# Rows of decays sent through DRAM and broadcast by DMA in place of selector products on TensorE

## The chip, the cores and the metric

The kernel runs on one core of a Trainium2 chip. The metric is the device time of one execution in microseconds (us). Before the change the median of three runs is 1075.29 us (1075.06 to 1076.16).

## The reference

One layer of a hybrid decoder, for a prompt of 512 tokens and 8 samples of 8 tokens each, width 1024, all in float32. After an RMS norm one projection gives the inputs of two recurrent mixers. The first is a Mamba-2 SSD with 16 heads (head size 64, state 128, 2 groups):

```
cum  = cumsum(lac)                                   # the decays of a chunk, per head
lmat = exp(where(causal, cum[t] - cum[s], -inf))
y_intra = (C_t . B_s) * lmat * dt_s   applied to x_s
y_inter = (C_t . h) * exp(cum[t])                    # h: state before the chunk
```

The second is an mLSTM with 4 heads (key 128, value 256), which has the same form with stabilised log gates: `dmat = exp(b[t] - b[s] + i[s] - m[t])` inside a chunk and `exp(b[t] + m_prev - m[t])` on the queries for the state. Both feed an output projection; then follow cross attention over 256 memory tokens and a SwiGLU, each with norms before and after. All new states are outputs too.

The part that matters here: for each head, one row of 512 numbers over the tokens (`cum` for SSD, `b - m` for mLSTM, called `sx`) must stand in all 128 partitions, since the matrix `cum[t] - cum[s]` has s on the partitions and t along the row. The exponential of the same row, for tokens 128 to 511, must stand in 64 partitions (SSD) or 128 (mLSTM).

## The kernel before, in words

Everything lies with features on the partitions and the 576 tokens (512 prompt, 64 sample) along the row. Projections go through `gemm` (L208): each float32 weight tile is split into a rounded part and a remainder (`split_w`, L178: a load into `raw` from SP's queue at L181, a cast on ScalarE at L191, a subtraction on VectorE at L198 or a DMA that accumulates at L196), and three matmuls (L215, L216, L218) make one product. `raw` has two buffers, the split weights three.

A scheduler sets the order on every engine at build time from a simulated timeline. Each engine, SP's DMA queue among them, then works strictly in that order and waits where something isn't ready. Hints in the code tie some instructions behind others (`issue_after`). One of them matters here: the matmuls of the value projection (`values`, L868, product at L882) are tied, by the list `steps_` at L925, behind the products of the SSD pairs (`inner[k]`, L712), so that they fill TensorE between the pairs in a written order. The projections of z are tied behind them in the same way (L1095, L1096).

Gates (L549 to L644, between about 60 and 95 us in the profile): the rows `cum` (16 heads) and `sx` (4 heads) are made in the pool `gates`, one row per partition. Lines 600 to 612 split each into three bfloat16 parts, stacked in `cumst` (80 x 576) and `sxst` (68 x 576); for each set of rows that is one memset on GpSimd, four operations on VectorE and three copies on ScalarE.

SSD of the prompt (`ssd_prompt`, L654, once for each of 2 groups): transposes, the products C.B (`cbs`), the states of the four chunks, and then 4 pairs of heads, 8 pairs in all. For each head of a pair, TensorE multiplies a selector column with `cumst` (L697), which puts the head's row into all 128 partitions of a PSUM bank `ps_l`. VectorE adds the negative decay of the partition and the causal mask, chunk by chunk, into `lm` (L700, four operations), ScalarE takes the exponential (L702), VectorE multiplies by `cbs` (L703). The tag `tmp` of `lm` has two buffers, so the two heads of a pair hold both. Matmuls make `ps_yi` from the pair (L710, 16 as recorded); after them the buffers are free. Then two more selector products (L715) put the pair's rows, tokens 128 to 511, into `ps_ec`, ScalarE takes their exponential into `ec` (L718, one buffer), VectorE multiplies by `ps_yn`, the product of the states (L723), and GpSimd adds to the output (L725).

mLSTM of the prompt (L957, 4 heads): a selector product with `sxst` (L960) gives `ps_d`; ScalarE takes its exponential into `qs` (L962), which GpSimd multiplies by the queries; VectorE adds gates and mask into `dm` (L966). `qs` and `dm` have two buffers each. The samples use the same stacks for tokens 512 to 575 (L780, L1013).

Of the kernel before, what the change touches and what calls it, by code (L numbers as in the profile page):

```python
# [11 lines left out]
F32 = mybir.dt.float32  # L12
F32R = mybir.dt.float32r
BF16 = mybir.dt.bfloat16
# [5 lines left out]
P = 128  # L20
T = 576
TP = 512
# [93 lines left out]
def build(nc, tc, ctx, I, O):  # L116
# [199 lines left out]
    c16 = ml.tile([P, NC16], BF16, name="c16")  # L316
    sel = C16("sel")
    CT = ml.tile([P, 5, 104], F32, name="CT")
    sxst = ml.tile([68, T], BF16, name="sxst")
    mrow = ml.tile([4, TS], F32, name="mrow")  # L320
    wendm = ml.tile([P, 5, 4], F32, name="wendm")
    scalem = ml.tile([P, 4, 4], F32, name="scalem")
# [121 lines left out]
    bcp = stb.enter_context(tc.tile_pool(name="bcp", bufs=1, reuse_waits="tile"))  # L444
    bc = bcp.tile([P, 4, T], F32, name="bc")
    cdup = bcp.tile([16, 2, TS], F32, name="cdup")
    cumst = bcp.tile([80, T], BF16, name="cumst")
    ncum = bcp.tile([P, 4, 16], F32, name="ncum")
    wend = bcp.tile([P, 5, 16], F32, name="wend")
    decp = bcp.tile([P, 4, 16], F32, name="decp")  # L450
# [98 lines left out]
    def row(name, n=68, dt=F32, tag=None):  # L549
        return gp_.tile([n, T], dt, name=name, tag=tag or name)  # L550
# [46 lines left out]
    V.tensor_copy(cdup, cum[0:16, TP:T].unsqueeze(1).to_broadcast([16, 2, TS]))  # L597
    A.copy(mrow, r2[:, TP:T])

    btt, d1t = row("btt", 48, BF16, tag="ig"), row("d1t", 48, tag="e1")  # L600
    for st_, src, n in ((cumst, cum[0:16, :], 16), (sxst, sx[r4, :], 4)):
        b0 = 32 if n == 4 else 0
        bt, d1 = btt[b0:b0 + n, :], d1t[b0:b0 + n, :]
        G.memset(st_, 0.0)
        V.tensor_copy(bt, src)
        A.copy(st_[0:n, :], bt)
        with tc.issue_after(sx_done.ins):
            V.tensor_tensor(d1, src, bt, op=ALU.subtract)
        V.tensor_copy(bt, d1)
        A.copy(st_[32:32 + n, :], bt)  # L610
        V.tensor_tensor(d1, d1, bt, op=ALU.subtract)
        A.copy(st_[64:64 + n, :], d1)
# [41 lines left out]
    def ssd_prompt(g):  # L654
        Bt, Ct = bc[:, g, :], bc[:, 2 + g, :]
        ps = MP("ps_bt")
        for c in range(4):
            TE.transpose(ps[:, c * P:(c + 1) * P], Bt[:, c * P:(c + 1) * P], ident)
        btok = sd.tile([P, 4, P], F32, name="btok", tag="btok")
        A.copy(btok, ps.rearrange("p (c k) -> p c k", c=4))  # L660
        ps = MP("ps_cb")
        for c in range(4):
            m = mm(ps[:, c * P:(c + 1) * P], Bt[:, c * P:(c + 1) * P], Ct[:, c * P:(c + 1) * P], start=True, stop=True,
                   skip_group_check=True)
        outer.append(m)
        cbs = sd.tile([P, 512], F32, name="cbs", tag="cbs")
        A.copy(cbs, ps)
        xdt, hs = [], [None]
        for c in range(4):
            ps = MP("ps_xt")  # L670
            for j in range(4):
                TE.transpose(ps[:, j * P:(j + 1) * P], xs[:, g * 4 + j, c * P:(c + 1) * P], ident)
            xd = sd.tile([P, 8, 64], F32, name="xdt", tag="xdt", bufs=4)
            V.tensor_tensor(xd, ps.rearrange("p (h k) -> p h k", h=8),
                            CT[:, c, 32 + 8 * g:40 + 8 * g].unsqueeze(2).to_broadcast([P, 8, 64]), op=ALU.mult)
            xdt.append(xd)
            xe = sd.tile([P, 8, 64], F32, name="xe", tag="xe", bufs=1)
# [12 lines left out]
        for j in range(4):  # L690
            jj = g * 4 + j
            psi = MP("ps_yi")
            lms = []
            for k in range(2):
                h = 2 * jj + k
                psb = MP("ps_l")
                mm(psb, sel[:80, h:h + 1].to_broadcast([80, P]), cumst[:, 0:TP], start=True, stop=True)  # L697
                lm = sd.tile([P, 512], F32, name="lm", tag="tmp", bufs=2)
                for c in range(4):
                    V.scalar_tensor_tensor(lm[:, c * P:(c + 1) * P], psb[:, c * P:(c + 1) * P], ncum[:, c, h:h + 1],  # L700
                                           C16("maskp"), op0=ALU.add, op1=ALU.add)
                exps.append(A.activation(lm, lm, AF.Exp))  # L702
                mults.append(V.tensor_tensor(lm, lm, cbs, op=ALU.mult))  # L703
                lms.append(lm)
                if len(mults) == 8:
                    G.tensor_copy(sd.tile([P, 1], F32, name="lm0"), lm[:, 0:1])

            for c in range(4):
                for k in (1, 0):
                    m = mm(psi[64 * k:64 * k + 64, c * P:(c + 1) * P], xdt[c][:, 2 * j + k, :], lms[k][:, c * P:(c + 1) * P],  # L710
                       start=True, stop=True, skip_group_check=True)
            inner.append(m)  # L712
            pse = MP("ps_ec")
            for k in range(2):
                mm(pse[64 * k:64 * k + 64, 0:384], sel[:80, 2 * jj + k:2 * jj + k + 1].to_broadcast([80, 64]),  # L715
                   cumst[:, P:TP], start=True, stop=True, skip_group_check=True)
            ec = sd.tile([P, 384], F32, name="ec", tag="ec", bufs=1)
            A.activation(ec, pse[:, 0:384], AF.Exp)  # L718
            psn = MP("ps_yn")
            for c in range(1, 4):  # L720
                mm(psn[:, (c - 1) * P:c * P], hs[c][:, 2 * j:2 * j + 2, :].rearrange("p h k -> p (h k)"),
                   Ct[:, c * P:(c + 1) * P], start=True, stop=True, skip_group_check=True)
            V.tensor_tensor(ec, ec, psn[:, 0:384], op=ALU.mult)  # L723
            V.scalar_tensor_tensor(y[:, jj, 0:TP], xs[:, jj, 0:TP], PAR("dskip", jj), psi, op0=ALU.mult, op1=ALU.add)
            G.tensor_tensor(y[:, jj, P:TP], y[:, jj, P:TP], ec, op=ALU.add)  # L725
# [50 lines left out]
    for g in range(2):  # L776
        psb = BP("ps_ls")
        pb3 = psb.rearrange("p (h t) -> p h t", h=8)
        for h in range(8):
            mm(psb[:, h * TS:(h + 1) * TS], sel[:80, 8 * g + h:8 * g + h + 1].to_broadcast([80, P]), cumst[:, TP:T],  # L780
               start=h == 0, stop=h == 7, skip_group_check=True)
# [174 lines left out]

    for h in range(4):  # L957
        q, k = qk[:, h, :], qk[:, 4 + h, :]
        psb = MP("ps_d")
        mm(psb, sel[:68, h:h + 1].to_broadcast([68, P]), sxst[:, 0:TP], start=True, stop=True)  # L960
        qs = mp_.tile([P, 384], F32, name="qs", tag="qs", bufs=2)
        A.activation(qs, psb[:, P:TP], AF.Exp)  # L962
        G.tensor_tensor(qs, qs, q[:, P:TP], op=ALU.mult)
        dm = mp_.tile([P, 512], F32, name="dm", tag="dm", bufs=2)
        for c in range(4):
            V.scalar_tensor_tensor(dm[:, c * P:(c + 1) * P], psb[:, c * P:(c + 1) * P], CT[:, c, 64 + h:65 + h],  # L966
                                   C16("maskp"), op0=ALU.add, op1=ALU.add)
        A.activation(dm, dm, AF.Exp)
        pss = MP("ps_s")
# [40 lines left out]
    psb = BP("ps_ds")  # L1010
    pb3 = psb[:, 0:256].rearrange("p (h t) -> p h t", h=4)
    for h in range(4):
        mm(psb[:, h * TS:(h + 1) * TS], sel[:68, h:h + 1].to_broadcast([68, P]), sxst[:, TP:T], start=h == 0, stop=h == 3,  # L1013
           skip_group_check=True)
    es = vt4_[:, 4128:4384].rearrange("p (h t) -> p h t", h=4)
    A.activation(es, pb3, AF.Exp)
# [1460 lines left out]
```

## Time and profile before

| | |
|---|---|
| median of the runs | 1075.29 us |
| the profiled execution | 1074.69 us |
| its span in the profile | 1072.9 us |
| granted TensorE clock, mean | 0.999 |
| moved by DMA | 181.74 MB, mean 169 GB/s |

The span is the stretch that the profile covers; the execution's own time is 1.8 us longer. PE is TensorE's matmul, PEld its weight load, DVE VectorE, ACT ScalarE, POOL GpSimd, SPq the queue on which SP issues DMAs. A row of a group gives line, engine, operation, output and inputs, shapes, count and durations. In views by time, the first column is the start in us from the beginning of the span, the second the duration of a merged piece, and a bracket at the end says how long the engine sat idle before it and what released it. In the chain of waits, the second column is the slot, the time that passed to the next piece. Matmuls are pipelined: the recorded duration of one is longer than its slot.

### The profile page before, as it was taken

To read this page: it belongs to the slowest core of one execution; us is meant where nothing else is said; L and a number is where in the kernel's file an instruction comes from. 1 tells how busy PE (TensorE), PEld (TensorE's weight loads), DVE (VectorE), ACT (ScalarE), POOL (GpSimd) and SP (SyncE) were. 2 spreads that over 40 slices of the span, in tenths; PEclk is the share of its full clock that TensorE was granted. 3 is DMA by queue.
4 is the path that set the end of the run, shared out by engine and by line. 5 is a ranking of instruction groups with operands and counts; after the bars stand their busy time and mean duration, and the time that the engine had idled before them with its cause. 6 is when DMAs were issued, how large, how long until landed. Compare 5 with 4: busy or idle time off the path is not lost.

```text
span 1072.9 us, 20686 instructions
## 1 busy us (share of the span) xinstructions
PE 1063.1 (99%) x8096; PEld 1011.0 (94%) x8096; DVE 757.7 (71%) x1523; ACT 608.9 (57%) x1102; POOL 231.0 (22%) x305
## 2 busy tenths in 40 slices
PE   9999999999999999999999999999999999999997
PEld 8999887778999999999999989999999999999997
DVE  6798775658878774758755556766467887787556
ACT  7778523345654555655555445645566566656654
POOL 0454543313213111000154201100011111111000
PEclk9999999999999999999999999999999999999999
DMA  6776544425655349642468775743476687578532
GB/s 209 176 162 132 158 134 172 147 89 168 196 150 152 106 143 330 235 170 98 158 213 288 265 256 176 254 124 98 133 179 137 160 188 178 114 191 188 144 119 89
DMA packets 58965, 181.74 MB, mean 169 GB/s; under 512 B 6604, under 2 KB 12108, under 8 KB 58356
## 3 DMA queue, kind: packets, MB, share of 16 engines
q1 hardware_dynamic: 42884, 138.22, 38.7%
q0 software_dynamic: 15408, 41.43, 19.7%
q8 instruction: 63, 1.03, 0.4%
q10 hardware_dynamic: 576, 0.79, 0.2%
q14 instruction: 34, 0.28, 0.1%
HBM read 159.75 MB, written 20.65 MB: 168 GB/s over the span
## 4 chain that ended last, share of the span: by engine, by line
PE 98%; DVE 0%; DMA 0%; POOL 0%; issue 0%; ACT 0%; SPq 0%; DVEq 0%
PE ps_in L215 7%; PE ps_in L218 7%; PE ps_in L216 7%; PE ps_v L882 5%; PE ps_g L1946 3%; PE ps_u L1946 3%; PE ps_g L1945 3%; PE ps_o L218 3%; PE ps_o L216 3%; PE ps_u L1947 3%; PE ps_g L1947 3%; PE ps_o L215 3%; PE ps_u L1945 3%; PE ps_dn L1945 2%; PE ps_dn L1947 2%; PE ps_dn L1946 2%
## 5 line engine op out<-in xcount | busy, mean ns | idle before, releaser
L215 PE MATMUL ps_in<-uh,whi 128*128 128x320 f32 (+1 forms) x544 | 162.6, 299 | 0.0
L218 PE MATMUL ps_in<-uh,wlo 128*128 128x320 f32 (+1 forms) x544 | 161.6, 298 | 0.0
L216 PE MATMUL ps_in<-ul,whi 128*128 128x320 f32 (+1 forms) x544 | 161.1, 296 | 0.0
L191 ACT CAST whi<-raw 128x1024 fp32r<-128x1024 f32 (+1 forms) x104 | 105.4, 1015 | 93.3 <-PE ps_in L216 21.5
L198 DVE TENSOR_TENSOR wlo<-raw,whi 128x1024 fp32r<-128x1024 f32 (+2 forms) x97 | 95.3, 983 | 63.7 <-ACT whi L191 63.0
L215 PEld LDWEIGHTS ps_in<-uh,whi 128*128 128x128 f32 x544 | 102.3, 188 | 1.9 <-issue 0.8
L218 PEld LDWEIGHTS ps_in<-uh,wlo 128*128 128x128 f32 x544 | 102.2, 188 | 1.9 <-issue 1.3
L216 PEld LDWEIGHTS ps_in<-ul,whi 128*128 128x128 f32 x544 | 102.4, 188 | 0.5
L196 POOL DMA_DIRECT2D wlo<-win x31 | 27.2, 877 | 80.2 <-ACT wlo L195 69.9
L1945 PE MATMUL ps_g<-b,whi 128*128 128x288 f32 x144 | 42.4, 295 | 0.0
L1946 PE MATMUL ps_g<-b,whi 128*128 128x288 f32 x144 | 42.3, 294 | 0.0
L1946 PE MATMUL ps_u<-b,whi 128*128 128x288 f32 x144 | 42.2, 294 | 0.0
L1945 PE MATMUL ps_u<-b,whi 128*128 128x288 f32 x144 | 42.2, 294 | 0.0
L1905 DVE TENSOR_TENSOR wlo<-sw,whi 128x1024 fp32r<-128x1024 f32 (+1 forms) x26 | 29.6, 1139 | 16.8 <-ACT whi L1904 16.8
L1918 ACT CAST whi<-rawx 128x1024 fp32r<-128x1024 f32 (+1 forms) x26 | 25.6, 986 | 26.2 <-PE ps_dn L1946 13.3
L1895 ACT CAST whi<-raw 128x1024 fp32r<-128x1024 f32 (+1 forms) x26 | 25.6, 985 | 22.8 <-PE ps_g L1946 11.8
L215 PE MATMUL ps_xo<-qh,whi 128*128 128x288 f32 x128 | 38.2, 301 | 0.0
L216 PE MATMUL ps_xo<-ql,whi 128*128 128x288 f32 x128 | 37.8, 297 | 0.0
L218 PE MATMUL ps_o<-mixm_h,wlo 128*128 128x256 f32 (+1 forms) x128 | 37.5, 293 | 0.0
L216 PE MATMUL ps_o<-mixm_l,whi 128*128 128x256 f32 (+1 forms) x128 | 37.5, 293 | 0.0
L218 PE MATMUL ps_xq<-u2h,wlo 128*128 128x320 f32 (+1 forms) x128 | 37.5, 294 | 0.0
L218 PE MATMUL ps_o<-mixs_h,wlo 128*128 128x320 f32 (+1 forms) x128 | 37.4, 293 | 0.0
(788 smaller groups left out, 3855.6 us busy)
## 6 DMA issues: line engine op xcount, KB each, us to landing
raw<-win SPq DMA_DIRECT2D x35, 512.0 KB, 4.4
raw<-wout SPq DMA_DIRECT2D x17, 512.0 KB, 4.2
raw<-wxq SPq DMA_DIRECT2D x13, 512.0 KB, 4.7
raw<-wgate SPq DMA_DIRECT2D x13, 512.0 KB, 3.3
raw<-wup SPq DMA_DIRECT2D x13, 512.0 KB, 4.7
wlo<-win POOLq DMA_DIRECT2D x24, 256.0 KB, 5.6
kva<-vc SPq DMA_DIRECT2D x11, 512.0 KB, 5.9
raw<-wv SPq DMA_DIRECT2D x10, 512.0 KB, 4.0
```

What stands on the lines that cost most here:

```text
L191: casts.append(A.copy(hi[:, :n], raw[:, :n]))
L196: accs.append(G.dma_start(lo[:, a:b], src[:, a:b], accum_op=ALU.add))
L198: e.tensor_tensor(lo[:, a:b], raw[:, a:b], hi[:, a:b].bitcast(F32), op=ALU.subtract)
L215: mm(ps, wh, ah, start=i == 0, stop=False)
L216: products.append(mm(ps, wh, al, start=False, stop=False))
L218: m = mm(ps, tiles[order[c]][1], xh(order[c], t0, n), start=False, stop=c == len(tiles) - 1)
L882: mm(ps, a, b, skip_group_check=True, **kw)
L1895: s.c1 = A.copy(s.h1[:, s.all], s.r1[:, s.all])
L1905: V.tensor_tensor(s.l2[:, s.all], sw[:, s.all], s.h2[:, s.all].bitcast(F32), op=ALU.subtract)
L1945: mm(ps, wh, b[0][k], start=start and k == 0, stop=False, skip_group_check=True)
L1946: mm(ps, wh, b[1][k], start=False, stop=False, skip_group_check=True)
L1947: m = mm(ps, wl, b[0][k], start=False, stop=k == nk - 1, skip_group_check=True)
```

## The change

The prompt's rows no longer go through the selector. Four DRAM tiles are added: `cum_d` (16 x 512), `ecum_d` (16 x 384), `sx_d` (4 x 512) and `esx_d` (4 x 384). ScalarE takes the exponentials of the rows once, ahead, into `ecr`; SP stores the four. Where `ps_l`, `ps_ec` and `ps_d` stood, SP now loads the row of a head, or of its exponential, broadcast over the partitions, straight into `lm`, `ec`, `qs` and `dm`; the additions of VectorE then work in place on SBUF. The stacks `cumst` and `sxst` shrink to the 64 sample tokens, and with them the conversions that fill them. `ecr` takes over the buffer `ig`, and `btt` gets one of its own.

```diff
-    sxst = ml.tile([68, T], BF16, name="sxst")
+    sxst = ml.tile([68, TS], BF16, name="sxst")
...
-    cumst = bcp.tile([80, T], BF16, name="cumst")
+    cumst = bcp.tile([80, TS], BF16, name="cumst")
...
-    btt, d1t = row("btt", 48, BF16, tag="ig"), row("d1t", 48, tag="e1")
-    for st_, src, n in ((cumst, cum[0:16, :], 16), (sxst, sx[r4, :], 4)):
+    cum_d, ecum_d, sx_d, esx_d = [dr.tile([n, w], F32, name=k) for n, w, k in
+                                  ((16, TP, "cum_d"), (16, 384, "ecum_d"), (4, TP, "sx_d"), (4, 384, "esx_d"))]
+    ecr = row("ecr", 36, tag="ig")
+    A.activation(ecr[0:16, 0:384], cum[0:16, P:TP], AF.Exp)
+    A.activation(ecr[r4, 0:384], sx[r4, P:TP], AF.Exp)
+    S.dma_start(cum_d, cum[0:16, 0:TP])
+    S.dma_start(ecum_d, ecr[0:16, 0:384])
+    S.dma_start(sx_d, sx[r4, 0:TP])
+    S.dma_start(esx_d, ecr[r4, 0:384])
+    btt, d1t = row("btt", 48, BF16, tag="btt"), row("d1t", 48, tag="e1")
+    for st_, src, n in ((cumst, cum[0:16, TP:T], 16), (sxst, sx[r4, TP:T], 4)):
...
-                psb = MP("ps_l")
-                mm(psb, sel[:80, h:h + 1].to_broadcast([80, P]), cumst[:, 0:TP], start=True, stop=True)
                 lm = sd.tile([P, 512], F32, name="lm", tag="tmp", bufs=2)
+                S.dma_start(lm, cum_d[h:h + 1, :].to_broadcast([P, TP]))
                 for c in range(4):
-                    V.scalar_tensor_tensor(lm[:, c * P:(c + 1) * P], psb[:, c * P:(c + 1) * P], ncum[:, c, h:h + 1],
+                    V.scalar_tensor_tensor(lm[:, c * P:(c + 1) * P], lm[:, c * P:(c + 1) * P], ncum[:, c, h:h + 1],
                                            C16("maskp"), op0=ALU.add, op1=ALU.add)
...
-            pse = MP("ps_ec")
+            ec = sd.tile([P, 384], F32, name="ec", tag="ec", bufs=1)
             for k in range(2):
-                mm(pse[64 * k:64 * k + 64, 0:384], sel[:80, 2 * jj + k:2 * jj + k + 1].to_broadcast([80, 64]),
-                   cumst[:, P:TP], start=True, stop=True, skip_group_check=True)
-            ec = sd.tile([P, 384], F32, name="ec", tag="ec", bufs=1)
-            A.activation(ec, pse[:, 0:384], AF.Exp)
+                S.dma_start(ec[64 * k:64 * k + 64, :], ecum_d[2 * jj + k:2 * jj + k + 1, :].to_broadcast([64, 384]))
...
-        psb = MP("ps_d")
-        mm(psb, sel[:68, h:h + 1].to_broadcast([68, P]), sxst[:, 0:TP], start=True, stop=True)
         qs = mp_.tile([P, 384], F32, name="qs", tag="qs", bufs=2)
-        A.activation(qs, psb[:, P:TP], AF.Exp)
+        S.dma_start(qs, esx_d[h:h + 1, :].to_broadcast([P, 384]))
         G.tensor_tensor(qs, qs, q[:, P:TP], op=ALU.mult)
         dm = mp_.tile([P, 512], F32, name="dm", tag="dm", bufs=2)
+        S.dma_start(dm, sx_d[h:h + 1, :].to_broadcast([P, TP]))
         for c in range(4):
-            V.scalar_tensor_tensor(dm[:, c * P:(c + 1) * P], psb[:, c * P:(c + 1) * P], CT[:, c, 64 + h:65 + h],
+            V.scalar_tensor_tensor(dm[:, c * P:(c + 1) * P], dm[:, c * P:(c + 1) * P], CT[:, c, 64 + h:65 + h],
                                    C16("maskp"), op0=ALU.add, op1=ALU.add)
```

The two lines for the samples (L780, L1013) read the whole of the smaller stacks.

More of the change, by code (lines that the diff above doesn't have):

```diff
@@ L598, in build @@
     A.copy(mrow, r2[:, TP:T])
-    btt, d1t = row("btt", 48, BF16, tag="ig"), row("d1t", 48, tag="e1")
-    for st_, src, n in ((cumst, cum[0:16, :], 16), (sxst, sx[r4, :], 4)):
+    cum_d, ecum_d, sx_d, esx_d = [dr.tile([n, w], F32, name=k) for n, w, k in
[9 more added lines that the diff above has]
+    for st_, src, n in ((cumst, cum[0:16, TP:T], 16), (sxst, sx[r4, TP:T], 4)):
         b0 = 32 if n == 4 else 0
-        bt, d1 = btt[b0:b0 + n, :], d1t[b0:b0 + n, :]
+        bt, d1 = btt[b0:b0 + n, 0:TS], d1t[b0:b0 + n, 0:TS]
         G.memset(st_, 0.0)
@@ L779, in build @@
         for h in range(8):
-            mm(psb[:, h * TS:(h + 1) * TS], sel[:80, 8 * g + h:8 * g + h + 1].to_broadcast([80, P]), cumst[:, TP:T],
+            mm(psb[:, h * TS:(h + 1) * TS], sel[:80, 8 * g + h:8 * g + h + 1].to_broadcast([80, P]), cumst,
                start=h == 0, stop=h == 7, skip_group_check=True)
@@ L1012, in build @@
     for h in range(4):
-        mm(psb[:, h * TS:(h + 1) * TS], sel[:68, h:h + 1].to_broadcast([68, P]), sxst[:, TP:T], start=h == 0, stop=h == 3,
+        mm(psb[:, h * TS:(h + 1) * TS], sel[:68, h:h + 1].to_broadcast([68, P]), sxst, start=h == 0, stop=h == 3,
            skip_group_check=True)
```

## The prediction

> **What bounds the kernel now.** I read the page first, then a table by stage over the part that the diff touches, then the chain of waits in that part, and last the order of VectorE's work there.
>
> ```profile
> span 1072.9 us, 20686 instructions
> PE 1063.1 (99%) x8096; PEld 1011.0 (94%) x8096; DVE 757.7 (71%) x1523; ACT 608.9 (57%) x1102; POOL 231.0 (22%) x305
> ```
>
> TensorE is busy for 1063.1 of 1072.9 us. Busy time alone says little when matmuls overlap, so the stage table (time; then busy us of PE, PEld, DVE, ACT, POOL; granted clock, share of the DMA engines, GB/s) is needed too:
>
> ```profile
> 130.00:160.00 30.00, 30.00 (x247) 25.93 (x246) 23.11 (x49) 9.79 (x17) 11.99 (x8) 1.00 0.43 130
> 160.00:190.00 30.00, 30.00 (x178) 22.11 (x177) 16.59 (x30) 9.00 (x14) 12.50 (x10) 1.00 0.45 159
> 190.00:220.00 30.00, 30.00 (x151) 22.85 (x150) 18.64 (x29) 10.08 (x14) 7.80 (x6) 1.00 0.43 149
> 220.00:260.00 40.00, 40.00 (x291) 34.70 (x290) 29.76 (x67) 24.75 (x40) 12.13 (x20) 1.00 0.46 141
> ```
>
> From 130 to 260 us, where the eight head pairs of the SSD run between projection products, PE has no gap at all, at full granted clock. The other engines have room, and the DMA engines are not half used. A matmul that is taken out here shortens the kernel by its slot, as long as the rest of the work stays in time for TensorE's fixed order.
>
> **What is removed.** Three kinds of selector products go. First their count (tile view), then their slots (chain of waits: start, us, work); a slot is what TensorE gives up, while the recorded duration overlaps its neighbours.
>
> ```profile
> L697 PE MATMUL ps_l<-cumst,c x16: 377/390/392, 129.4 to 243.8; 80*128 80x512 bf16 x16
> L715 PE MATMUL ps_ec<-cumst,c x16: 327/328/328, 138.9 to 248.2; 80*64 80x384 bf16 x16
> L960 PE MATMUL ps_d<-sxst,c x4: 380/381/383, 249.3 to 343.3; 68*128 68x512 bf16 x4
> ```
> ```profile
> 215.88 0.17 PE ps_ec L715 x2
> ...
> 221.08 0.45 PE ps_l L697 x2
> ```
>
> Two of the ps_l take 0.45 us, so 16 take 16 x 0.22 = 3.5 us. The two halves of ps_ec run side by side, 0.17 for both, so eight pairs take 8 x 0.165 = 1.3. Four of ps_d, of the same width, take 4 x 0.22 = 0.9. The sum is 5.7 us. The upper end adds the time in which the weight load before ps_l sat idle (its line's view says `issue`), if that goes as well:
>
> ```profile
>   issue: 2.6, 10
> ```
>
> That is PEld's idle time, most of it under running matmuls, so I do not take it; it makes the best case 8.3.
>
> ScalarE loses twelve exponentials and VectorE nothing but its wait for PSUM. The additions and masks keep their count and shapes and only read SBUF in place of PSUM; I cost that at nothing, VectorE having 7 to 13 us free in each stage above. The PSUM banks that are set free may help the order, and I count nothing for it.
>
> **What is added: the refills.** The rows go out once by four stores, early: the decays are there when their conversion starts (72.1, a row further below), long before the first ps_l at 129.4. SP then issues 16 broadcasts of 128 x 512 floats for lm, 16 of 64 x 384 for ec, four of 128 x 512 for dm and four of 128 x 384 for qs: 4.2 + 1.6 + 1.0 + 0.8 = 7.6 MB. Over some 215 us (129 to 343) that is 35 GB/s beside the 130 to 159 in the table, which fits shares of 0.43 to 0.46. Transfers as such are not the matter; latency is.
>
> For dm and qs there are two buffers, and the four heads lie 31 us apart (249.3 to 343.3): hidden. The one ec buffer is free from the add of one pair to the product of the next, and the pairs lie 9 us or more apart (below): hidden unless the queue is stuck. The lm buffers are the tight case. There are two, one pair needs both, and both are held until that pair's last product. Where PE could put the next rows into PSUM ahead of that, the new DMA cannot be issued before it. So: how long is it today from the last product of a pair (ps_yi) to the first addition (L700) of the next? First the chain of waits, then VectorE in order of time:
>
> ```profile
> 138.03 1.02 PE ps_yi L710 x16
> ...
> 152.35 1.02 PE ps_yi L710 x16
> ...
> 214.85 1.02 PE ps_yi L710 x16
> ...
> 227.71 1.02 PE ps_yi L710 x16
> ...
> 238.52 1.02 PE ps_yi L710 x16
> ...
> 247.32 1.07 PE ps_yi L710 x16
> ```
> ```profile
> 143.52 1.13 DVE L700 SCALAR_TENSOR_TENSOR lm<-ps_l,ncum,c 128x128 f32<-128x128 f32 x4 [2.78 <-PE ps_l L697]
> 150.88 0.68 DVE L703 TENSOR_TENSOR lm<-lm,cbs 128x512 f32<-128x512 f32 x1
> 156.97 2.15 DVE L700 SCALAR_TENSOR_TENSOR lm<-ps_l,ncum,c 128x128 f32<-128x128 f32 x8
> 167.52 2.16 DVE L700 SCALAR_TENSOR_TENSOR lm<-ps_l,ncum,c 128x128 f32<-128x128 f32 x8 [1.40 <-PE ps_l L697]
> 221.35 2.16 DVE L700 SCALAR_TENSOR_TENSOR lm<-ps_l,ncum,c 128x128 f32<-128x128 f32 x8 [3.78 <-PE ps_l L697]
> 234.19 2.16 DVE L700 SCALAR_TENSOR_TENSOR lm<-ps_l,ncum,c 128x128 f32<-128x128 f32 x8 [1.34 <-PE ps_l L697]
> 243.61 2.16 DVE L700 SCALAR_TENSOR_TENSOR lm<-ps_l,ncum,c 128x128 f32<-128x128 f32 x8 [2.38 <-PE ps_l L697]
> 245.69 1.47 DVE L703 TENSOR_TENSOR lm<-lm,cbs 128x512 f32<-128x512 f32 x2
> ```
>
> The six gaps are 143.52 - 139.05 = 4.5, then 3.6, 5.5 (the one whose pair is not shown), 5.5, 5.5 and 4.1 us. (The first pair of each group finds its buffers free long before.) Behind them lies a second reserve: from the end of the pair's last mask product (L703) to its ps_yi. At the first it is 152.35 - 151.56 = 0.8, at the last 247.32 - 247.16 = 0.2; the six, in order, are 0.8, 0.1, 0.9, 2.3, 0.8, 0.2. A refill that lands within gap plus reserve, 5.3, 3.7, 6.3, 7.8, 6.2 and 4.2 us after its release, costs TensorE nothing. How long will it take? No such DMA is in the trace; these are the nearest (KB, median us from issue to landing):
>
> ```profile
> raw<-wv SPq DMA_DIRECT2D x10, 512.0 KB, 4.0
> c<-c SPq DMA_DIRECT2D x8, 516.0 KB, 6.7
> ...
> o_ssmp<-hs SPq DMA_DIRECT2D x2, 256.0 KB, 3.0
> ```
>
> The 256 KB store lands in 3.0 us, and a pair of lm is as much as one 512 KB load, 4.0. The second lm is needed only 1.1 us after the first (four additions), so the pair should do as today. I take 3.0 for the first and 4.0 for the second, by size: nothing late. The upper end is 6.7, the longest row; the lower end, below nothing, would be an earlier chain, but TensorE, already full, could not run faster by it. The Trainium skill, DMA: Bandwidth & Descriptors, section "Anatomy of one DMA", fits 2.0 us plus bytes over 436 GB/s; by it 256 KB take an estimated 2.6 us, and the sum stays as it is. No run here shows that fit for this size; the row above says 3.0.
>
> **What is added and moved early on.** The two exponentials over the rows come where the conversions stand, from 72 us on, among casts and SiLUs. Each can cost a change of ScalarE's table there and back:
>
> ```profile
> 80.00:90.00 10.00, 10.00 (x68) 8.61 (x67) 9.75 (x23) 9.62 (x16) 4.76 (x10) 1.00 0.82 110
> ```
> ```profile
> 90.04 1.28 ACT L635 ACT_TABLE_LOAD   x1
> ```
> ```profile
> L606 ACT COPY cumst<-btt x1: 672/672/672, 72.1 to 72.1; 16x576 bf16<-16x576 bf16 x1
> ```
>
> Four loads are 5.1 us, the two exponentials about 0.6 each by the 0.67 of a row this wide. Against it stand six copies of 576 columns (0.67 each) that shrink to 64: by columns alone 0.6 each, 3.6 in all; some of a copy is fixed, so an estimate of half, 1.8, is nearer. At worst ScalarE gets 5.1 + 1.2 - 1.8 = 4.5 us more work in a stage where it is busy 9.62 of 10; at best, with no table load, 2.4 less. VectorE, at 9.75 of 10, gets its eight operations on those rows shortened the same way, which is a relief. Weights are converted a tile or more ahead, so I take no cost on TensorE. The stores are four SP issues among loads that wait for buffers anyway.
>
> **The sum.** The profiled execution took 1074.69 us, so 1074.69 - 5.7 = 1069.0; it lay 0.6 below the median of the runs, so 1069.6 beside 1075.29.
>
> **Rivals.** First, slower: SP, being in order, has a refill standing behind a weight load that waits for its buffer. In the stretch from 60 to 360 us:
>
> ```profile
> SPq L181 <- DVE wlo L198: 100.1, 23, 14.4
> ```
>
> The mean wait is 100.1 / 23 = 4.35 us. With one such wait ahead of each of the six tight refills the first lm lands 7.35 us after its release, late by 2.1, 3.6, 1.0, 0, 1.1 and 3.1: 11.0 us. TensorE cannot fill that in, since a written order ties the value products behind the pairs (L881). Result 1069.6 + 11.0 = 1080.6. It decides where release to landing passes 6.3 us, at which the lateness eats the 5.7. For it: SP waits this way often. Against: the scheduler that fixes SP's order gives the earlier-written lm precedence when its buffer is free.
>
> Second, slower still: the gaps above cannot be used, because the scheduler fills them with other VectorE work and the landing is exposed in full. Each refill then costs 3.0 less the reserve: 2.2 + 2.9 + 2.1 + 0.7 + 2.2 + 2.8 = 12.9, so 1082.5. The Trainium skill, DMA: Bandwidth & Descriptors, section "Rules for kernel authors", asks for a DMA to be issued early and waited for late; two buffers for a pair do not allow that here. Against: VectorE stood idle in five of the six gaps, 1.3 to 3.8 us, waiting for ps_l.
>
> Third, no change: refills take the 6.7 of the slowest row, late by 1.4, 3.0, 0.4, 0, 0.5 and 2.5 = 7.8 us, so 1077.4, just within what counts as no change. Against: an lm has half the bytes.
>
> Fourth, also no change: ScalarE's table loads delay converted weights by the full 4.5, so 1074.1. Against: it takes both changes of table, and a TensorE that is out of weights at once.
>
> **How the numbers follow.** What a measurement can tell from no change is about 0.2%, 2.15 us. Forecast 0.50 (faster); refills behind SP's waits 0.22 and exposed landing 0.08 (slower, 0.30 together); slow landing 0.12 and table loads 0.08 (within, 0.20 together). The range runs from 1067.0 (the 2.6 us of weight-load idle gone too) to 1081.0, past the first rival; only the second lies beyond. The forecast's own range is 1067.0 to 1072.
>
> **What would show it.** Right: PE's count lower by 36, no PE gap from 130 to 355, waits of VectorE for ps_l replaced by like waits for the DMA of lm, release to landing of lm 3 to 4 us, pairs about as far apart as now. Wrong: PE idle before ps_yi, released by L703 or lm; SP waits ahead of the lm broadcasts; landings over 6 us; new table loads between 68 and 90 us with PE waiting on whi or wlo. If PE is dense and the time has not fallen, other products would have grown, and my view of slots would be wrong.

## The result, and the profile after

| | before | after |
|---|---|---|
| median of 6 runs each | 1075.82 us (1075.06 to 1076.96) | 1092.76 us (1090.43 to 1094.43) |
| the profiled execution | 1074.69 us | 1090.43 us |
| its span | 1072.9 us | 1088.7 us |
| granted TensorE clock, mean | 0.999 | 0.991 |

The ratio is 1.0156, with a 95% interval of 1.0143 to 1.0169: the change makes the kernel slower by 16.8 us. The prediction said 1069.6, and 1081.0 at the upper end. In the two profiled executions nearly all of the loss lies between 80 and 400 us: the first product of the gates' transposes (`ps_ct`) is 0.6 us later than before, the first of the output projection (`ps_o`) 15.3 us (384.1 before, 399.4 after), and the cross attention still 15.2 (496.7, 511.9). The whole span is 15.8 us longer; the last 0.6 us come later.

The head of the page of the kernel after:

```profile
span 1088.7 us, 20696 instructions
PE 1068.7 (98%) x8060; PEld 1014.3 (93%) x8060; DVE 761.3 (70%) x1523; ACT 606.4 (56%) x1096; POOL 230.7 (21%) x305
```

TensorE has its 36 products fewer (8060 beside 8096), yet it is busy for 5.6 us longer, and idle for 20.0 us (1088.7 - 1068.7) beside 9.8. The stage table, in the columns of the prediction, shows where:

```profile
130.00:160.00 30.00, 26.21 (x229) 21.89 (x230) 21.34 (x36) 7.27 (x12) 14.89 (x12) 0.97 0.42 124
160.00:190.00 30.00, 30.00 (x175) 25.07 (x176) 19.45 (x37) 7.38 (x11) 3.85 (x5) 0.91 0.58 189
190.00:220.00 30.00, 29.93 (x138) 20.15 (x137) 17.24 (x23) 9.84 (x13) 15.52 (x11) 1.00 0.58 191
220.00:260.00 40.00, 38.59 (x260) 32.53 (x258) 27.89 (x56) 18.55 (x28) 10.30 (x16) 1.00 0.64 177
```

Before, all of these had PE full and a clock of 1.00. Now PE stands still for 3.8 us in the first stretch, and in the second, where it is busy all the time, the clock is 0.91. The waits of PE from 60 to 420 us (what waited, for what: us in all, times, longest) name the stops; before, this view was empty:

```profile
PE ps_yi L718 <- DVE lm L711: 3.8, 1, 3.8
PE ps_in L215 <- DVE tmp L1093: 2.3, 1, 2.3
PE ps_in L215 <- DVE tmp L1137: 0.9, 1, 0.9
PE ps_hts L1078 <- DVE hns L1075: 0.9, 1, 0.9
PE ps_en L634 <- ACT CT L628: 0.8, 1, 0.8
PE ps_nh L1053 <- DMA c<-c: 0.7, 2, 0.4
PE ps_ct L626 <- ACT r L595: 0.3, 1, 0.3
```

A stop can cost more than its length. TensorE's own order of time around the longest:

```profile
155.83 0.28 PE L215 MATMUL ps_in<-uh,whi 128*128 128x256 f32 x1
159.89 1.97 PE L718 MATMUL ps_yi<-lm,xdt 128*64 128x128 f32 x16 [3.79 <-DVE lm L711]
...
163.88 0.41 PE L218 MATMUL ps_in<-uh,wlo 128*128 128x256 f32 x1
164.10 0.41 PE L215 MATMUL ps_in<-uh,whi 128*128 128x256 f32 x1
...
165.43 0.28 PE L216 MATMUL ps_in<-ul,whi 128*128 128x256 f32 x1
165.54 0.28 PE L218 MATMUL ps_in<-uh,wlo 128*128 128x256 f32 x1
```

Behind the stop the projection's products start 0.22 us apart and are recorded with 0.41; from 165.2 on they are 0.11 apart, with 0.28. For 5.3 us TensorE ran at half rate, so 2.6 us went on top of the 3.8. Over the stages from 60 to 400 us the shares of the clock that are missing from 1.00 add up to 6.8 us, beside 9.7 us of stops: 16.5 together, and 10.8 when the 5.7 us of slots that went are taken off. This counts a little twice: the record of half rate around this stop runs from 158.38 to 165.21 us, and until 159.89 TensorE stood still. The other 4.4 of the 15.2, and some 0.7 more for what is counted twice, lie spread over slots that grew without a stop, and come back under what stays open.

Now the cause of the long stop. VectorE and GpSimd in order of time, after:

```profile
149.06 1.14 DVE L708 SCALAR_TENSOR_TENSOR lm<-lm,ncum,c 128x128 f32<-128x128 f32 x4 [1.81 <-DMA lm<-cum_d]
150.12 0.68 DVE L801 TENSOR_TENSOR xs<-yds,ps_yis 128x512 f32<-128x512 f32 x1
150.71 6.18 DVE L708 SCALAR_TENSOR_TENSOR lm<-lm,ncum,c 128x128 f32<-128x128 f32 x4
150.91 7.78 POOL L826 TENSOR_TENSOR h<-h,vt 128x1024 f32<-128x1024 f32 x4 [1.94 <-PE ps_hs L818]
157.15 2.68 DVE L711 TENSOR_TENSOR lm<-lm,cbs 128x512 f32<-128x512 f32 x2
```

The refill was 1.81 us late for VectorE, as the prediction expected of it. Then four additions take 1.14 us, and the next four, of the same shape, 6.18: those run while GpSimd multiplies `h`. Of the four, the first took 0.35 us and the other three 2.02 to 2.03. The mask product at 157.15 took 2.08. And the same beside the same work before the change:

```profile
141.80 8.08 POOL L821 TENSOR_TENSOR h<-h,vt 128x1024 f32<-128x1024 f32 x4
...
146.00 2.07 DVE L703 TENSOR_TENSOR lm<-lm,cbs 128x512 f32<-128x512 f32 x1
```

There the additions that read `ps_l` from PSUM kept their 0.34 us (143.52, 1.13 for four, shown ahead of the result), but the mask product, which reads both its inputs from SBUF, took 2.07 in place of 0.68. So a slowed mask product occurs without the change too; the slowed additions do not. The price of moving an input to SBUF stood in the trace of before, between two rows that the prediction quoted.

The tile view of `lm` and of `dm`, after (count, then ns min/median/max; then us and times that an engine sat idle until that DMA; then release to landing):

```profile
L708 DVE SCALAR_TENSOR_TENSOR lm<-lm,ncum,c x64: 339/346/2032, 110.5 to 248.3; 128x128 f32<-128x128 f32 x64
...
  DMA lm<-cum_d: 10.2, 7
...
DMA to landing us min/median/max: 3.1/3.5/6.0
```
```profile
  DMA dm<-sx_d: 7.3, 4
...
DMA to landing us min/median/max: 3.4/4.0/7.5
```

The landings are what was forecast, and VectorE waits 10.2 us for `lm`'s DMA where it had waited 11.7 for `ps_l`. Only the maximum of 2032 ns shows what went wrong; the median of the additions is nearly unchanged (346 ns, 340 before).

### The profile page after: what moved, and what is told of

It reads as the page before. It is cut to its first block, busy times and chain, and to the rows that moved or that the text cites. A ratio compares the mean times of both kernels' runs of the same rounds, so it can differ in the third digit from the quotient of the medians.

```text
span 1088.7 us, 20696 instructions
## 1 busy us (share of the span) xinstructions
PE 1068.7 (98%) x8060; PEld 1014.3 (93%) x8060; DVE 761.3 (70%) x1523; ACT 606.4 (56%) x1096; POOL 230.7 (21%) x305
## 4 chain that ended last, share of the span: by engine, by line
PE 83%; DMA 6%; DVE 5%; ACT 2%; issue 1%; POOL 1%; SPq 1%; DVEq 0%; ACTq 0%
PE ps_in L215 4%; PE ps_in L218 4%; PE ps_v L887 4%; PE ps_in L216 4%; PE ps_g L1950 3%; PE ps_u L1950 3%; PE ps_g L1949 3%; PE ps_o L218 3%; PE ps_o L216 3%; PE ps_u L1951 3%; PE ps_g L1951 3%; PE ps_u L1949 3%; PE ps_o L215 3%; PE ps_dn L1949 2%; PE ps_dn L1951 2%; PE ps_dn L1950 2%
## 5 line engine op out<-in xcount | busy, mean ns | idle before, releaser
L191 ACT CAST whi<-raw 128x1024 fp32r<-128x1024 f32 (+1 forms) x104 | 105.1, 1014 | 115.4 <-PE ps_in L216 27.2
L216 PE MATMUL ps_in<-ul,whi 128*128 128x320 f32 (+1 forms) x544 | 163.6, 301 | 0.0
L215 PE MATMUL ps_o<-mixm_h,whi 128*128 128x256 f32 (+1 forms) x128 | 37.4, 292 | 0.0
```

The source lines that it names most:

```text
L191: casts.append(A.copy(hi[:, :n], raw[:, :n]))
L215: mm(ps, wh, ah, start=i == 0, stop=False)
L216: products.append(mm(ps, wh, al, start=False, stop=False))
```

## The experiments

Theory A, formed from these rows: latency of the refills is not the matter; the loss is (1) additions that slow down beside GpSimd, (2) early exponentials that make ScalarE load tables ahead of `CT`, (3) waits and order on VectorE around the start of the mLSTM, each enlarged by the half rate. The rival: the round trip through DRAM is too slow for the two `lm` buffers. All runs are in one table; "over" is (ratio - 1) x 1075.8 us. The ratio is estimated from runs of both kernels made together, so it need not be the quotient of the medians.

| kernel | median, us | ratio (95% interval) | over, us |
|---|---|---|---|
| the change | 1092.76 | 1.0156 (1.0143 to 1.0169) | 16.8 |
| 1 SSD half alone | 1087.60 | 1.0116 (1.0091 to 1.0141) | 12.5 |
| 2 mLSTM half alone | 1081.83 | 1.0056 (1.0041 to 1.0071) | 6.0 |
| 3 stores and exponentials alone | 1080.28 | 1.0047 (1.0031 to 1.0063) | 5.1 |
| 4 change, exponentials later | 1091.23 | 1.0139 (1.0124 to 1.0154) | 15.0 |
| 5 change, GpSimd held back | 1087.23 | 1.0101 (1.0081 to 1.0121) | 10.9 |
| 6 additions in SBUF, no DMA | 1089.56 | 1.0130 (1.0110 to 1.0149) | 14.0 |
| 7 change, three `lm` buffers | 1091.41 | 1.0130 (1.0102 to 1.0158) | 14.0 |
| 8 `ec` alone | 1076.03 | 1.0001 (0.9993 to 1.0010) | 0.1 |
| 9 SSD half, two mends | 1082.02 | 1.0057 (1.0040 to 1.0075) | 6.1 |
| 10 mLSTM half, exponential later | 1080.33 | 1.0043 (1.0027 to 1.0060) | 4.6 |
| 11 stores alone, exponentials later | 1076.10 | 1.0001 (0.9990 to 1.0012) | 0.1 |
| 12 SSD half, three mends | 1074.54 | 0.9991 (0.9982 to 1.0000) | -1.0 |
| 13 before, selector products twice | 1082.17 | 1.0055 (1.0039 to 1.0072) | 5.9 |
| 14 change, three mends | 1081.21 | 1.0046 (1.0031 to 1.0060) | 4.9 |

**1 and 2. The halves.** In the first the mLSTM keeps `ps_d`, in the second the SSD keeps `ps_l` and `ps_ec` (against the change, one of the places of each):

```diff
+        psb = MP("ps_d")
+        mm(psb, sel[:68, h:h + 1].to_broadcast([68, P]), sxst[:, 0:TP], start=True, stop=True)
-        S.dma_start(dm, sx_d[h:h + 1, :].to_broadcast([P, TP]))
```
```diff
+                psb = MP("ps_l")
+                mm(psb, sel[:80, h:h + 1].to_broadcast([80, P]), cumst[:, 0:TP], start=True, stop=True)
-                S.dma_start(lm, cum_d[h:h + 1, :].to_broadcast([P, TP]))
```

> Only the SSD's rows (lm and ec) go through DRAM; the mLSTM keeps its selector products. Theory A (three separate stalls: table loads early on, the lm refill of the second pairs with its slow additions beside GpSimd, the late dm of the mLSTM): the stall near 155 us and one of the two early table changes stay, those near 260 and 320 us go, so about half of the 17 us: 1082 to 1086 us. Theory B (the new order as a whole costs, no part by itself): the parts do not add up; 1090 or more, or near 1076, with gaps in other places. Theory C (latency of the refill on its own): the same as the change, about 1090, with gaps before ps_yi in every pair.

> Only the mLSTM's rows (dm and qs) go through DRAM; the SSD keeps its selector products. Theory A: VectorE waits for dm near 255 and 315 us as in the change, TensorE stops there and runs at half clock behind it: 5 to 8 us over the kernel before, 1080 to 1084 us, and none of the stall near 155. Theory B: anything, with gaps elsewhere. Theory C: as the kernel before within 2 us, since two buffers hide the latency.

12.5 and 6.0 us, 18.5 together, beside 16.8 for the whole (its interval is 1.4 either way). The long stop at 157 us (3.9) with additions of 2019 to 2036 ns belongs to the SSD half, and so does one of 2.9 at 259 us; the mLSTM half has one of 2.5 at 88 us and small ones later, and of its additions to `dm` the slowest took 0.74 us. By the first products behind that stop, 4.4 us of the mLSTM half's loss are there by 100 us, where the table loads of experiment 3 act, and not at the mLSTM.

**3 and 11. What is stored, read by nobody.** Before, with the rows stored and the exponentials taken, and the products left as they were:

```diff
+    A.activation(ecr[0:16, 0:384], cum[0:16, P:TP], AF.Exp)
+    A.activation(ecr[r4, 0:384], sx[r4, P:TP], AF.Exp)
+    S.dma_start(cum_d, cum[0:16, 0:TP])
...
```

Kernel 11 takes the two exponentials and stores them after line 640 instead, beside those that already stood there.

> The kernel before, with all its selector products, plus the two exponentials over the rows and the four stores, which nothing reads. Theory A: the two exponentials bring two changes of ScalarE's table, 5.1 us of ScalarE near 70 and 85 us, the copy of CT comes 3 us later and TensorE stops there: 2 to 4 us over the kernel before, 1078 to 1080. Rival: ScalarE has room, no more than 0.5 us: 1076.

> The kernel before plus the two exponentials in the group near 91 us and the four stores, which nothing reads. Theory A (the table changes made the 4 us of the run with early exponentials): as the kernel before, 1075 to 1076.5. Rival (the stores, or the order that they bring, cost): 1078 to 1081.

5.1 us against 0.1: the stores cost nothing, the place of the exponentials does. The chain of waits of the change shows how (start, us):

```profile
80.50 1.28 ACT L604
81.80 0.53 ACT ecr L604
...
84.72 1.28 ACT L526
86.01 0.63 ACT xs L526
...
87.35 0.52 ACT CT L628
87.91 0.96 PE ps_en L634 x2
```

The two pieces of 1.28 without a tile are table loads, to the exponential and back for the SiLU. `CT` is copied at 87.35; before it was at 84.02. In kernel 3 the stop at `ps_en` is 2.3 us, and between 60 and 420 us nothing else stops. Its profiled execution is 5.2 us longer in span than before. Of these, 2.9 are there behind the stop (the first `ps_xt` at 98.5 before and 101.4 in kernel 3) and stay 2.9 at the output projection; the rest arises between 600 and 740 us, where the edit changes nothing, and no run explains it.

**4. The change with the exponentials later**, moved as in kernel 11, to where ScalarE takes exponentials anyway (their two stores follow them):

```diff
-    A.activation(ecr[0:16, 0:384], cum[0:16, P:TP], AF.Exp)
-    A.activation(ecr[r4, 0:384], sx[r4, P:TP], AF.Exp)
...
+            A.activation(ecr[0:16, 0:384], cum[0:16, P:TP], AF.Exp)
+            A.activation(ecr[r4, 0:384], sx[r4, P:TP], AF.Exp)
```

> The change, with the two exponentials moved into the group of exponentials near 91 us, and their two stores behind them. Theory A: no more table loads than in the kernel before, no stop of TensorE at 80 to 90 us: 2.5 to 4 us under the change, 1089 to 1090. Rival (table loads lie beside other work, the stop there has another cause): as the change, 1092 to 1093.

15.0, that is 1.8 us under the change, with overlapping intervals. The stop at 88 us is gone, and others grew (4.3 at 159, 2.1 at 325). In the change that stop was only 0.8, yet the delay there was like kernel 3's: TensorE had already run at half rate from 83.29 to 86.70, and its first `ps_xt` came at 101.7, 3.2 us later than before. So the traces put about 3 us on the table loads, with or without the rest of the change; by whole times it is 5.1 alone, with what the trace leaves unexplained, and 1.8 within the change, which is less than that difference is uncertain by.

**5. GpSimd held back.** The change, with the multiplications of `h` for the first two samples tied behind the third pair's mask products, by a copy of one column on GpSimd:

```diff
-            with tc.issue_after(mults[7].ins) if b == 2 else ExitStack():
+            with tc.issue_after(mults[7].ins) if b == 2 else tc.issue_after(held[0].ins) if b < 2 else ExitStack():
```

> The change, with GpSimd's four products over the sample states (h with decs, 2 us each, near 151 us in the change) held back until the masks of the third pair are multiplied, so that they no longer run beside that pair's additions. Theory A (additions that read SBUF on VectorE are slowed to 2 us by GpSimd's work on SBUF, and that makes the stop near 155 us): additions of the third pair at 0.34 us each, that stop of 3.8 us gone or under 1 us, 4 to 7 us under the change: 1086 to 1089 us. Theory C (the stop is the refill's latency): additions fast, yet the stop and the time stay within 1.5 us of the change.

10.9: 5.9 us less than the change, within the 1086 to 1089 that was expected. The stop near 160 us is gone; of 64 additions one took 1741 ns and one 1097, the rest about 346. These two too ran beside GpSimd, and TensorE did not stop for them: a slow addition costs something only where the reserve is small. The 5.9 are net of another stop, which was larger in this kernel than in the change (2.3 us at `ps_en`, in place of 0.8).

**6. The additions in SBUF without any DMA.** Before, with one line more: ScalarE copies `ps_l` into `lm`, and the additions work in place.

```diff
+                A.copy(lm, psb)
-                    V.scalar_tensor_tensor(lm[:, c * P:(c + 1) * P], psb[:, c * P:(c + 1) * P], ncum[:, c, h:h + 1],
+                    V.scalar_tensor_tensor(lm[:, c * P:(c + 1) * P], lm[:, c * P:(c + 1) * P], ncum[:, c, h:h + 1],
```

> The kernel before, selector products and all, no DMA added; only that ScalarE first copies ps_l to lm and VectorE adds in place on SBUF, as in the change. Theory A: additions that fall beside GpSimd's products over the sample states take up to 2 us in place of 0.34, TensorE stops near 150 us; 3 to 8 us over the kernel before: 1079 to 1084. Theory C (only the DMA's latency counts): the copies lie on an idle ScalarE and the additions stay at 0.34 us; 1076 to 1078.

14.0 us, with no row through DRAM. GpSimd and VectorE in order of time:

```profile
141.90 7.73 POOL L822 TENSOR_TENSOR h<-h,vt 128x1024 f32<-128x1024 f32 x4
...
144.98 6.11 DVE L701 SCALAR_TENSOR_TENSOR lm<-lm,ncum,c 128x128 f32<-128x128 f32 x8 [0.69 <-ACT lm L699]
```

Eight additions take 6.11 us where eight took 2.16; the three that overlap GpSimd took 0.90, 2.02 and 2.03, and from GpSimd's end on each took 0.34. That shows the slowdown without the change's DMAs. The kernel's whole loss is more than A expected (1079 to 1084 us). TensorE stops there for 5.4 us, in four pieces, for VectorE's `h`, and for 2.9, in three, for `lm`. The copies also stand in the chain, and I did not take the two apart.

**7. A third buffer.**

```diff
-                lm = sd.tile([P, 512], F32, name="lm", tag="tmp", bufs=2)
+                lm = sd.tile([P, 512], F32, name="lm", tag="tmp", bufs=3)
```

> The change with three lm buffers in place of two, so that the first refill of a pair can start a pair earlier. Theory C: half of the exposed latency goes; VectorE's waits for lm (14 us in the change) fall to half and the time by 4 us or more, to under 1089. Theory A: the waits fall, the slow additions and the late dm stay; within 2 us of the change, 1091 to 1094.

14.0, with an interval of 11.0 to 17.0 that overlaps the change's, 15.4 to 18.2. VectorE still waits for the refills, 7.3 us in place of 10.2, so this run alone speaks only weakly against the rival. Kernel 12 below decides it for the SSD half: with two buffers and the rows through DRAM, VectorE waits 16.4 us for the refills of `lm` there, more than in the change, and the kernel loses nothing.

**8. Only `ec`** through DRAM, with its exponential late, against the kernel before:

```diff
-            A.activation(ec, pse[:, 0:384], AF.Exp)
+            for k in range(2):
+                S.dma_start(ec[64 * k:64 * k + 64, :], ecum_d[2 * jj + k:2 * jj + k + 1, :].to_broadcast([64, 384]))
```

> The kernel before, with only ec through DRAM (its exponential taken once, in the group near 91 us), and lm and the mLSTM by selector products. ec has a whole pair's time to land and no operand of VectorE moves from PSUM to SBUF. Theory A: no new stop; the eight ps_ec slots of 0.165 us are gained: 1.3 us under the kernel before, 1074.5 to 1075.5. Theory B (any new order costs): 1078 or more.

One stop of 0.3 us, and no gain either: 0.1 us (interval -0.8 to 1.1), where 1.3 us of slots are gone.

**13. The price of a slot.** Before, each of the removed products issued twice, into the same bank:

```diff
+                mm(psb, sel[:80, h:h + 1].to_broadcast([80, P]), cumst[:, 0:TP], start=True, stop=True)
...
-            for k in range(2):
+            for k in (0, 1, 0, 1):
...
+        mm(psb, sel[:68, h:h + 1].to_broadcast([68, P]), sxst[:, 0:TP], start=True, stop=True)
```

> The kernel before with every selector product that the change removes issued twice into the same bank (16 ps_l, 16 ps_ec, 4 ps_d more). If the slots as read from the chain of waits are their worth, 5.7 us more: 1080.5 to 1081.5. If the slots lie partly over time that TensorE would lose to its neighbours anyway (the run with only ec through DRAM gained nothing for 1.3 us of slots), 0 to 3 us more: 1075.5 to 1078.5.

5.9 us more (interval 4.2 to 7.7) for 36 further products. The chain of waits, start and slot, lines 697 and 698 being the product and its double:

```profile
224.49 0.23 PE ps_l L697
224.72 0.21 PE ps_l L698
...
231.93 0.33 PE ps_ec L716 x4
```

0.22 for one `ps_l`, 0.165 for two `ps_ec`: the 5.7 us of the prediction's sum were priced rightly. The 5.9 hold two short stops too, of 0.6 and 0.3 us, which lie well within the interval.

**9 and 12. The SSD half with its causes taken away.** Kernel 9 is kernel 1 with the edits of kernels 4 (for the SSD's row) and 5.

> The SSD's rows through DRAM as in the change, with the exponential in the group near 91 us, GpSimd's four products over the sample states held back behind the third pair, and the mLSTM by selector products: every part whose harm is shown is taken out. Theory A: no stop near 85, 155 or 320 us; what is left of the chain's lateness (refills of 3.5 us in place of rows made ahead in PSUM) costs up to 4 us: 1073 to 1080 us, about as the kernel before. Theory B: the new order alone costs, so still 1085 or more.

6.1, half of kernel 1, and one stop left: 3.1 us at 252.6 us, `ps_in` waiting for VectorE's `tmp`. VectorE in order of time:

```profile
245.36 0.55 DVE L726 TENSOR_TENSOR ec<-ec,ps_yn 128x384 f32<-128x384 f32 x1
247.06 0.42 DVE L1022 TENSOR_TENSOR ds__3138<-ps_ds,CT 64x256 f32<-64x256 f32 x1 [1.15 <-POOL xs L728]
247.40 0.27 DVE L1066 TENSOR_TENSOR m4t<-c32e,mrow 4x128 f32<-4x128 f32 x1
247.60 1.11 DVE L969 SCALAR_TENSOR_TENSOR dm<-ps_d,CT,c 128x128 f32<-128x128 f32 x4
...
252.18 0.80 DVE L1092 SCALAR_TENSOR_TENSOR tmp<-tmp,ps_in 128x256 f32<-128x256 f32 x2
```

The operation that frees z's PSUM banks (L1092) stands behind work for the mLSTM and the samples; before, it came straight after the last `ec`, at 250.01 to that one's 249.54. The order is the scheduler's, and the change altered it. Kernel 12 gives z's first operations precedence:

```diff
+            with tc.high_priority(offset=1000) if j == 0 else ExitStack():
```

> The run before it (SSD's rows through DRAM, late exponential, GpSimd's products held back, mLSTM by selector), with the evacuation of the first z tile given precedence, so that on VectorE it stands ahead of the first mLSTM head's work as in the kernel before, and no longer five operations behind it. Theory A, completed (what is left there is one stop of 3.1 us near 252, TensorE out of PSUM banks for z, and half clock behind it): that stop goes, 3 to 6 us under the run before it: 1076 to 1079 us. Theory B (many small losses all over the new order): within 1.5 us of the run before it, 1080.5 to 1083.5.

```profile
245.53 0.55 DVE L726 TENSOR_TENSOR ec<-ec,ps_yn 128x384 f32<-128x384 f32 x1
...
247.77 0.40 DVE L1093 SCALAR_TENSOR_TENSOR tmp<-tmp,ps_in 128x256 f32<-128x256 f32 x1
```

That is worth 7.1 us for a stop of 3.1: behind the stop kernel 9's products started 0.27 us apart for 6.2 us, which is another 3.1 us lost; the clock from 220 to 260 us was 0.91 in kernel 9 and is 1.00 here. The SSD half is now at 0.9991 of the kernel before, best of all, though its interval touches 1. It has slow additions too (one of 2.03 us at 210 us), and TensorE does not stop for them.

**10 and 14. The mLSTM half.** Kernel 10 is kernel 2 with the edit of kernel 4 (for the mLSTM's row); kernel 14 is the whole change with the edits of kernels 4, 5 and 12.

> Only the mLSTM's rows through DRAM, with their exponential in the group near 91 us. Theory A: the stop near 88 us of the run with only the mLSTM changed goes, the waits of VectorE for dm stay: 1 to 4 us over the kernel before, 1077 to 1080. Theory C: nothing left, 1075 to 1076.

> The whole change, mLSTM rows by DMA too, with the three mends: exponentials in the group near 91 us, GpSimd's products held back, z's first evacuation ahead. Theory A: only VectorE's waits for dm (near 260 and 315 us) are left over the best run so far, 2 to 5 us: 1076.5 to 1080, 13 to 16 us under the change. Rival: the waits of the refills add up after all, 1083 or more.

Kernel 10 loses 4.6 us. Kernel 14 loses 4.9, that is 11.9 less than the change and 5.9 more than kernel 12, which differs from it by the mLSTM half. What that half waits for, in kernel 14 (tile view of `dm`, then VectorE in order of time):

```profile
  DMA dm<-sx_d: 11.8, 4
...
DMA to landing us min/median/max: 7.4/7.5/7.6
```
```profile
308.67 0.41 DVE L1096 SCALAR_TENSOR_TENSOR tmp<-tmp,ps_in 128x256 f32<-128x256 f32 x1
315.91 1.14 DVE L972 SCALAR_TENSOR_TENSOR dm<-dm,CT,c 128x128 f32<-128x128 f32 x4 [6.83 <-DMA dm<-sx_d]
```

For 6.83 us VectorE does nothing at all, since the additions of `dm` are next in its order. This is the last head: the buffer came free when its last reader, a `ps_n` product, began at 306.5, the request went out at 308.32, and the row landed 7.5 us later, while VectorE had been ready from 309.1 on. TensorE stops three times in that half, for `c<-c` each time, 3.9 us in all; the longest, 2.1, ends at 314, before VectorE's wait does, so it is no consequence of that wait. For the first two heads the requests go out in a bunch, shown by SP's queue in the change:

```profile
247.66 6.84 SPq L181 DMA_DIRECT2D raw<-win  x3
254.54 0.42 SPq L965 DMA_DIRECT2D qs<-esx_d  x1
255.06 0.39 SPq L968 DMA_DIRECT2D dm<-sx_d  x1
255.50 0.43 SPq L965 DMA_DIRECT2D qs<-esx_d  x1
256.01 0.85 SPq L968 DMA_DIRECT2D dm<-sx_d  x1
```

The rows of two heads are requested within 2 us, behind three weight loads and ahead of the loads of `c`, though they have been in DRAM since before 90 us. No run mends this half, so what part of the 5.9 us comes from `dm`, from the loads of `c` and from the half rate behind the stops (and, in the profiled execution, at 83 us) is not shown.

## Why the prediction was wrong

**The step that failed** is the sentence that the additions and masks "only read SBUF in place of PSUM; I cost that at nothing". An addition that meets GpSimd's multiplication costs 2.02 us in place of 0.34, and three such, where the pair had little reserve, made the stop of 3.8 us that broke TensorE's run. Kernel 5, which keeps GpSimd away, loses 5.9 us less, and kernel 6 shows the slow additions without a DMA. Free time on VectorE was no cover: the pair's whole reserve behind that gap was 0.1 us by the prediction's own list.

**dm and qs "hidden"** failed too. Two buffers and heads 31 us apart say when a request may go out, not when it does. It goes out late, for the first two heads in a bunch and for the last only when its buffer came free, and VectorE waits in order: 7.3 us in the change, 11.8 in kernel 14. This is the mechanism of the first rival, in a place where it was not looked for. That VectorE waits is shown; what TensorE loses by it is not.

**Table loads: "I take no cost on TensorE".** The time on ScalarE was right (four new loads in pairs), the victim wrong: not the converted weights, but `CT`, which waits in ScalarE's order. Alone 5.1 us by the whole time and 2.9 by the trace at that place; within the change 1.8 by the whole time and about 3 by the trace.

**The order of other work** was no term of the sum. The prediction went by pair and buffer and did not ask what the scheduler would do with z's first operations at 250 us: 7.1 us (kernel 12 against 9).

**What a stop costs.** The rivals counted lateness as time. TensorE often ran at half rate as well, for 3.4 to 6.2 us after a stop where I measured it, which made 7.1 us of a stop of 3.1. Not every stop brought this: kernel 3's of 2.27 us, at 85.6, did not.

**Right:** the slots, 5.7 us priced and 5.9 measured by doubling; the landings of 3 to 4 us (3.5) in the gaps, with VectorE's wait for the DMA in place of that for `ps_l`; the stores for nothing. The second rival's exposed landing made VectorE wait for `lm`, but by kernel 12 this costs TensorE nothing.

**The sum of the causes.** Measured as differences: table loads 1.8, additions beside GpSimd 5.9, order at z 7.1, mLSTM half 5.9, less the 1.0 that kernel 12 gains: 19.7 against 16.8. The parts overlap, as one stop lies in another's shadow, and each difference has an interval of 1 to 3 us either way, so they are not a partition. The first three are differences between a kernel with the cause and one without it; the mLSTM half's is what is left when the others are mended.

**Open.** Kernel 12 has 4.8 us of slots less than before and 1.2 us of stops between 10 and 420 us, but gains 1.0; kernel 8 gains nothing for 1.3. Adding products costs their slots; taking them out does not give the slots back in full. By the slots up to the output projection, in kernel 12 some neighbours are longer than before (`ps_hs` by 1.0 us, `ps_yi`, `ps_hu` and `ps_c` by 0.7 to 0.8 each), while others are shorter (`ps_v` by 1.7, `ps_in` by 1.2). It may be that the removed products had covered something there; no run tests that.

## What to carry to other kernels

When an operand moves from PSUM to SBUF, look in the trace for the longest time, not the median, of an operation whose inputs already lie in SBUF, and see what GpSimd does beside it. On engines that work in a fixed order, a DMA in place of a product is hidden only if its request goes out early and the waiting instruction has nothing urgent behind it; a second buffer alone does not see to that. A product taken off a full TensorE brings at most its slot, while taking away the cause of a stop of 3.8 us gained 5.9 here, and of one of 3.1, 7.1, so the first question about such a change is which stop it may cause.

## What the runs showed of the hardware

- **VectorE beside GpSimd.** In the change the three additions at 150.98, 152.93 and 154.88 us took 2032, 2021 and 2019 ns, and each ended 0.15 us after one of GpSimd's multiplications did (1957 to 1981 ns each); the same distance holds for the slow ones of kernels 5, 6 and 12. The end of GpSimd's instruction sets the time, and the width adds little to it: a 128x512 mask product took 2081 and ended 0.55 us after GpSimd's. The Trainium skill, SBUF — State Buffer, section "Who interferes with whom", says that a VectorE instruction with two SBUF inputs contends with a GpSimd instruction that reads SBUF, and that the one issued second waits for the whole of the other; one with at most one SBUF input, outside the two-port modes, does not. The traces agree: with `ps_l` in PSUM the additions took 0.34 us beside the same GpSimd work, with `lm` in SBUF and the mask as the second input 2.02. GpSimd is delayed in turn: before the change, its multiplication at 147.48, which met the mask product of 146.00, took 2394 ns, where those ahead of it start 1.9 us apart.
- **TensorE after a stop.** After 2.27 us of standing still at 258.6 to 260.9 the products of 320 columns started 0.265 us apart until 264.2, and 0.146 after that: 3.4 us at half rate. The Trainium skill, TensorE: Matmul & The Clock Gate, section "What's actually happening", gives just two rates, with about 3.4 us of steady work needed for the full one; behind this stop the trace agrees with both. Behind two longer stops, of 3.8 us in the change and 3.1 in kernel 9, the half rate lasted 5.3 and 6.2 us. The section sets an idle window of about 3.4 us for the fall. Here the rate also fell behind stops of 2.27 us (at 258.6) and of 0.26 (at 80.4, half rate from 83.29), and it did not fall behind one of 2.27 in kernel 3, so the length of a stop alone does not tell.
- **A row broadcast to 128 partitions by DMA** (256 KB) landed in 3.1, 3.5 and 6.0 us (least, median, most) for `lm` in the change. When `qs` and `dm` were requested in a bunch, `qs` (192 KB) took 3.8, 7.4 and 8.7 there, and in kernel 14 `dm` (256 KB) 7.4 to 7.6. The fit that the prediction named gives an estimated 2.6 us; its section states it for DMAs issued from GpSimd, and these went out from SP's queue.
